# A two-layer diffusion block on one core: scan block copies in runs, the state decayed on GpSimd, adaLN vectors as products by rows

## The chip, the cores and the metric

The kernel runs on one core of one Trainium2 chip. Its engines are TensorE (PE, with its weight loads PEld), VectorE (DVE), ScalarE (ACT), GpSimd (POOL) and SyncE (SP), whose queue issues the DMAs. The metric is the device time of one execution in microseconds.

## The reference

The program computes two layers over 512 latent tokens and 256 context tokens of width 1024. Layer 0 mixes the tokens by a bidirectional RWKV-7 recurrence, layer 1 by a Hyena long convolution, and each layer has a SwiGLU feed-forward on either side. All of it is float32. Every sub-layer is steered by shift, scale and gate vectors (adaLN), nine per layer, which one linear map of SiLU(c) gives; in layer 0 the context has its own from SiLU(c_ctx).

```python
ml = [m[:, None, :] for m in jnp.split(jax.nn.silu(c) @ mod_w[i] + mod_b[i], 9, axis=-1)]
mc = jnp.split(jax.nn.silu(c_ctx) @ mod_w[i] + mod_b[i], 9) if ctx_live else None
xl = xl + 0.5 * ml[2] * _swiglu(_pre(xl, norm_g[i, 0], ml[0], ml[1]), ffn_w_gu[i, 0], ffn_w_down[i, 0])
...
def step(S, inp):
    w_t, k_t, v_t, kk_t, ka_t = inp[:5]
    sa = jnp.einsum('dbhvk,dbhk->dbhv', S, kk_t)
    S = S * w_t[..., None, :] - sa[..., None] * ka_t[..., None, :] + v_t[..., None] * k_t[..., None, :]
```

## The kernel before, in words

Activations lie transposed, features on the partitions. Each float32 product is made of three products of halves (`mm3`, lines 470 to 473): a weight block is loaded raw by SP (`wfetch`), split into `whi` on ACT and `wlo` on DVE (`split`, lines 476 and 477), and used by TensorE. The raw pool has two buffers, so SP issues a weight load when the block two before it has been split.

A feed-forward (`ffn`) goes through the hidden width in parts of 4 (first one) or 8 and 6 blocks. For each pair of hidden blocks TensorE makes gate and up products, ACT and DVE form `dh` and `dl`; then the part's down products are added into the residual `x` by DVE with the gate vector (line 594, and 647 in the page). PSUM has a pool of eight buffers. Between pairs and between down blocks `bg_step` advances the background work.

That work is the adaLN vectors but the first two: (layer, vector) (0,2) to (0,4) for both streams and (0,5) to (0,8) for latents in the first feed-forward, (1,0) to (1,4) in the second, (1,5) to (1,8) in the third. For one vector `mod_dve` loads eight blocks of 128 rows of the map into `mraw` (two buffers, `mod_raw`, line 373), and DVE adds each, scaled by the stream's SiLU(c), into an accumulator `macc` of 128x1024 (lines 406 and 408). Eight matmuls against a column of ones then sum the accumulator over the partitions (line 414; each is recorded twice) and `mod_place` adds the bias.

The recurrence runs in chunks of 64 tokens, 12 blocks of two chunks, both directions. In each block the triangular matrices `Bc` are copied block by block into `Dl` (`lanes`, ACT, line 1223), transposed in 32x32 squares on DVE into `L` (`lanes2`, 1227), inverted on DVE (1258, 1265), transposed back (`unlane`, 1277) and copied into `XT` (`unlane2`, ACT, 1288). The state `Sn` is carried by `carry`: DVE writes the decayed state into the operand `SV` of a later step (1337) and GpSimd then decays `Sn` itself (1338); `advance` adds the new part (1376). `scores` has its lower half masked by GpSimd (1175) after ACT copied it out (1174).

A scheduler that simulates the program orders most of it. In the first blocks of the scan PE, DVE and POOL keep the written order, later PE and DVE, and in the adaLN vectors of the start PE; each engine runs its instructions in the order so found, SP's DMA issues too.

## Time and profile before

| | us |
|---|---|
| three runs | 3077.65, 3083.25, 3086.89; median 3083.25 |
| profiled execution | 3075.51 |
| its span | 3073.7 |
| busy: PE, DVE, ACT, POOL | 2822.9, 1811.0, 1203.1, 434.7 |
| mean granted TensorE clock | 0.944 of 2.4 GHz |

The span counts from the first to the last instruction. A row of a view by line groups all instructions of one source line and shape; "idle before" is the time its engine sat still before them and what ended it. Waits are inferred, and an engine's idle time matters only where another waits for it.

### The profile page before, as it was taken

What the parts mean: (1) busy time and instruction counts of PE and PEld (TensorE: products, weight loads), DVE (VectorE), ACT (ScalarE), POOL (GpSimd) and SP (SyncE); (2) the same over time, 40 slices, a digit from 0 to 9 for tenths busy, and PEclk for the clock granted to TensorE, in tenths of its full rate; (3) what the DMA queues carried; (4) which work ended last, traced back from release to release, by engine and by line L of the source; (5) the groups of instructions that cost most, each with busy time, mean ns of one, the idle gap of its engine ahead of it and who ended that gap; (6) DMA issues with size and microseconds to landing.
All of it is one profiled execution on the core that took longest, in us unless ns stands there. A gap on an engine that the chain in (4) does not pass through costs nothing.

```text
span 3073.7 us, 46929 instructions
## 1 busy us (share of the span) xinstructions
PE 2822.9 (92%) x18698; PEld 2362.3 (77%) x18698; DVE 1811.0 (59%) x3253; ACT 1203.1 (39%) x2003; POOL 434.7 (14%) x515
## 2 busy tenths in 40 slices
PE   8999999968889577887899999999999989899998
PEld 4888888857666466766788889888887767888888
DVE  5744544373798678887745555454356578653334
ACT  3121121254667788884232223322234322242222
POOL 0000000032343445432100000000000044100000
PEclk9999999989999678889899999999999999999999
DMA  6533432312688734324535444354233444332231
GB/s 226 175 105 116 151 103 83 95 40 99 173 211 213 192 106 135 109 83 120 189 110 172 146 162 144 103 186 156 96 118 121 179 169 151 107 110 96 96 101 50
DMA packets 363394, 407.28 MB, mean 133 GB/s; under 512 B 77655, under 2 KB 303063, under 8 KB 361448
## 3 DMA queue, kind: packets, MB, share of 16 engines
q1 hardware_dynamic: 363176, 404.29, 42.0%
q8 instruction: 147, 2.41, 0.3%
q14 instruction: 71, 0.58, 0.1%
HBM read 338.10 MB, written 65.34 MB: 131 GB/s over the span
## 4 chain that ended last, share of the span: by engine, by line
PE 75%; DVE 11%; ACT 6%; DMA 4%; issue 3%; POOL 1%; SPq 0%; DVEq 0%; ACTq 0%; POOLq 0%
PE ps L471 21%; PE ps L473 21%; PE ps L472 21%; PE sc L1198 1%; PE ps L414 1%; ACT Dl L1223 1%; DVE wlo L477 1%; ACT XT L1288 1%; DVE Dl L1265 1%; ACT AG L1174 1%; DVE xm L743 1%; DVE Tm L1258 1%; PE pf L1747 1%; DVE SV L1337 1%; DVE zt L1934 1%
## 5 line engine op out<-in xcount | busy, mean ns | idle before, releaser
L472 PE MATMUL ps<-hl,whi 128*128 128x512 f32 (+1 forms) x2064 | 742.0, 362 | 3.8 <-DVE hl L265 3.7
L471 PE MATMUL ps<-hh,whi 128*128 128x512 f32 (+1 forms) x2064 | 733.0, 363 | 13.1 <-ACT hh L264 10.7
L473 PE MATMUL ps<-hh,wlo 128*128 128x512 f32 (+1 forms) x2064 | 735.9, 362 | 2.6 <-DVE wlo L477 2.6
L477 DVE TENSOR_TENSOR wlo<-raw,whi 128x1024 fp32r<-128x1024 f32 (+1 forms) x325 | 393.0, 1215 | 404.0 <-ACT whi L476 402.7
L476 ACT CAST whi<-raw 128x1024 fp32r<-128x1024 f32 (+1 forms) x338 | 344.7, 1028 | 719.4 <-PE ps L472 657.0
L471 PEld LDWEIGHTS ps<-hh,whi 128*128 128x128 f32 x2064 | 386.8, 191 | 76.9 <-ACT hh L264 13.3
L472 PEld LDWEIGHTS ps<-hl,whi 128*128 128x128 f32 x2064 | 392.6, 190 | 64.3 <-DVE hl L265 5.1
L473 PEld LDWEIGHTS ps<-hh,wlo 128*128 128x128 f32 x2064 | 391.6, 190 | 64.6 <-DVE wlo L477 3.7
L472 PE MATMUL ps<-dl,whi 128*128 128x512 f32 (+1 forms) x1072 | 357.6, 335 | 0.0
L473 PE MATMUL ps<-dh,wlo 128*128 128x512 f32 (+1 forms) x1072 | 356.9, 334 | 0.0
L471 PE MATMUL ps<-dh,whi 128*128 128x512 f32 (+1 forms) x1072 | 356.2, 336 | 0.0
L601 DVE TENSOR_TENSOR sg<-sg,ps 128x512 f32<-128x512 f32 (+1 forms) x110 | 69.2, 633 | 259.1 <-PE ps L473 249.8
L408 DVE SCALAR_TENSOR_TENSOR macc<-mraw,cs,macc 128x1024 f32<-128x1024 f32 x133 | 169.0, 1283 | 87.9 <-DMA mraw<-in_mod_w 87.2
L471 PEld LDWEIGHTS ps<-dh,whi 128*128 128x128 f32 x1072 | 203.3, 190 | 20.9
L473 PEld LDWEIGHTS ps<-dh,wlo 128*128 128x128 f32 x1072 | 203.7, 190 | 20.4
L472 PEld LDWEIGHTS ps<-dl,whi 128*128 128x128 f32 x1072 | 203.7, 190 | 20.0
L600 ACT ACTIVATE sg<-ps 128x512 f32<-128x512 f32 (+1 forms) x110 | 59.7, 553 | 228.9 <-PE ps L473 216.3
L476 ACT CAST dh<-sg 128x512 fp32r<-128x512 f32 (+1 forms) x110 | 62.4, 576 | 213.5 <-DVE sg L601 213.4
L1779 POOL TENSOR_SCALAR G<-G 128x512 f32<-128x512 f32 x8 | 11.9, 1492 | 938.2 <-ACT G L1770 920.5
L472 PE MATMUL ps<-xl,whi 128*128 128x512 f32 (+2 forms) x336 | 124.8, 373 | 11.5 <-DVE xl L798 6.7
L647 DVE SCALAR_TENSOR_TENSOR x<-ps,der,x 128x512 f32<-128x512 f32 (+1 forms) x128 | 82.4, 664 | 81.6 <-PE ps L473 81.5
L471 PE MATMUL ps<-xh,whi 128*128 128x512 f32 (+1 forms) x336 | 120.9, 372 | 9.8 <-ACT xh L805 6.5
(313 smaller groups left out, 4619.8 us busy)
## 6 DMA issues: line engine op xcount, KB each, us to landing
raw<-in_wgu SPq DMA_DIRECT2D x88, 1024.0 KB, 5.0
mraw<-in_mod_w SPq DMA_DIRECT2D x144, 512.0 KB, 4.3
raw<-in_wd SPq DMA_DIRECT2D x24, 1024.0 KB, 4.7
raw<-in_wrkv SPq DMA_DIRECT2D x12, 1024.0 KB, 5.7
S_A<-AR SPq DMA_DIRECT2D x32, 384.0 KB, 3.6
AG<-S_A SPq DMA_DIRECT2D x48, 256.0 KB, 4.4
KK<-S_K SPq DMA_DIRECT2D x24, 512.0 KB, 4.5
KL<-S_K SPq DMA_DIRECT2D x48, 256.0 KB, 2.9
```

Of the source, the lines that this page charges most:

```text
L408: nc.vector.scalar_tensor_tensor(acc, raw, sc, acc, ALU.mult, ALU.add)
L414: nc.tensor.matmul(pt[:, m : m + 1], acc[:, m * P : (m + 1) * P], self.ones, start=m == 0, stop=m == DT - 1)
L471: nc.tensor.matmul(out, wh, xh, start=start, stop=False)
L472: nc.tensor.matmul(out, wh, xl, start=False, stop=False)
L473: nc.tensor.matmul(out, wl, xh, start=False, stop=stop)
L476: self.nc.scalar.copy(hi, src)
L477: (self.nc.gpsimd if pool else self.nc.vector).tensor_tensor(lo, src, hi.bitcast(F32), ALU.subtract)
L600: nc.scalar.activation(sg, pg, AF.Silu)
L601: nc.vector.tensor_mul(sg, sg, pu)
L647: nc.vector.scalar_tensor_tensor(X[m][:, o : o + w], pt, gates[who][:, m : m + 1], X[m][:, o : o + w], ALU.mult, ALU.add)
L743: nc.vector.scalar_tensor_tensor(dst, src, self.pv(f"mix{j}")[:, mc], dst, ALU.mult, ALU.add)
L1174: nc.scalar.copy(dst, src)
```

## The change

The adaLN map's columns from the third vector on are handed over transposed (`mod_wt`), so that one row of 1024 inputs belongs to one output. `mod_rows` spreads SiLU(c) (and SiLU(c_ctx)) as a row over all partitions: a column copy on GpSimd, a DMA that repeats the row, and a Silu of 128x1024 on ACT, once per feed-forward with background work. `mod_dve` multiplies each block of 128 outputs by that row and sums along it in one DVE instruction, whose sums are a column of the vector; the matmuls against ones are gone. Each load waits for a one-column copy on GpSimd that reads `begun`, the last `dl` written. In the scan the copies to `Dl` and to `XT` run over 32 neighbours, and the two transposes take the permutation instead. GpSimd decays the state first, and DVE copies it to `SV`.

```diff
-        if (i, k) == (0, 2) and q < self.nmod:
-            self.nc.vector.tensor_copy(raw[:, :1], self.begun)
-        self.nc.sync.dma_start(raw, self.A["mod_w"][i, q * P : (q + 1) * P, k * D : (k + 1) * D])
+        if held is not None:
+            self.nc.gpsimd.tensor_copy(raw[:, :1], held)
+        self.nc.sync.dma_start(raw, src)
...
+    def mod_rows(self, whos):
+        nc = self.nc
+        self.rows = {}
+        for w in whos:
+            t = self.rows[w] = self.modp.tile([P, D], F32, tag=f"mc{w}", name=self.nm("mc"))
+            nc.gpsimd.tensor_copy(t[:, :1], self.begun)
+            nc.sync.dma_start(t, self.A["cv"][("l", "c").index(w) : ("l", "c").index(w) + 1].to_broadcast([P, D]))
+            nc.scalar.activation(t, t, AF.Silu)
...
-            raw = self.mod_raw(i, k, q)
-            for w, acc in zip(whos, accs):
-                sc = self.cs[:, q, (0 if w == "l" else 1)].unsqueeze(1)
-                if q == 0:
-                    nc.vector.tensor_scalar(acc, raw, sc, None, ALU.mult)
-                else:
-                    nc.vector.scalar_tensor_tensor(acc, raw, sc, acc, ALU.mult, ALU.add)
+            raw = self.mod_raw(self.A["mod_wt"][i, o : o + P], self.begun)
+            for j, w in enumerate(whos):
+                dst = raw
+                if j < len(whos) - 1:
+                    dst = self.modp.tile([P, D], F32, tag="mprod", name=self.nm("mprod"))
+                nc.vector.tensor_tensor_reduce(
+                    dst, raw, self.rows[w], 1.0, 0.0, ALU.mult, ALU.add, accum_out=cols[w][:, m : m + 1]
+                )
...
-        for w, acc in zip(whos, accs):
-            pt = self.ps(DT)
-            for m in range(DT):
-                nc.tensor.matmul(
-                    pt[:, m : m + 1], acc[:, m * P : (m + 1) * P], self.ones, start=m == 0, stop=m == DT - 1
-                )
-            self.mod_place(pt, w, i, k)
+        for w in whos:
+            self.mod_place(cols[w], w, i, k)
...
+                    self.begun = dl[-1][:, :1].bitcast(F32)
+                    if jp == 0 and self.bg:
+                        self.mod_rows(("l", "c") if first else ("l",))
                     self.bg_step(4 if first and j0 == 0 else 2)
...
-            BD = t["BD"] = Dl.rearrange("p a r -> p (a r)").rearrange("p (t c) -> p t c", c=16)
-                nc.scalar.copy(BD[r].rearrange("p t c -> p c t"), Bcc[r, :, b : b + 32])
+                nc.scalar.copy(Dl[r], Bcc[r, :, b : b + 32])
...
-                L.rearrange("p r (h c) -> p r h c", h=2), t["BD"].unsqueeze(2).to_broadcast([P, 32, 2, 16])
+                L.rearrange("p r (h c) -> p r h c", h=2),
+                Dl.rearrange("p c t -> p t c").unsqueeze(2).to_broadcast([P, 32, 2, 16]),
...
-            nc.vector.transpose(XD, Dl)
-            t["XD"] = XD.rearrange("p a (h c) -> p a h c", h=2)
+            nc.vector.transpose(XD.rearrange("p c (a h) -> p a h c", h=2), Dl.rearrange("p a (h c) -> p a h c", h=2))
...
-                nc.scalar.copy(XTc[r, :, b : b + 32], t["XD"][r].rearrange("p a h c -> p c (a h)"))
+                nc.scalar.copy(XTc[r, :, b : b + 32], t["XD"][r])
...
+            nc.gpsimd.tensor_tensor(Sn, Sn, pc.to_broadcast([P, NP, 64]), ALU.mult)
             for hh in range(2):
-                nc.vector.tensor_mul(SV[hr[hh], hh], Sn[hr[hh]], pc[hr[hh]].to_broadcast([64, NP, 64]))
-            nc.gpsimd.tensor_tensor(Sn, Sn, pc.to_broadcast([P, NP, 64]), ALU.mult)
+                nc.vector.tensor_copy(SV[hr[hh], hh], Sn[hr[hh]])
```

SP's queue at the first part of the first feed-forward, before: `raw` are weight blocks (`in_wd` the down projection's), `mraw` blocks of the adaLN map; 654 to 668 stand ahead of these rows, and the vector (0,2) ends with 928.

```order
L450 DMA raw_680<-in_wgu 128x8x256
L373 DMA mraw_916<-in_mod_w 128x1024
L450 DMA raw_690<-in_wd 128x4x256
L373 DMA mraw_920<-in_mod_w 128x1024
L373 DMA mraw_924<-in_mod_w 128x1024
L373 DMA mraw_928<-in_mod_w 128x1024
L373 DMA mraw_1018<-in_mod_w 128x1024
L373 DMA mraw_1022<-in_mod_w 128x1024
L450 DMA raw_958<-in_wd 128x4x256
L450 DMA raw_1030<-in_wd 128x4x256
L450 DMA raw_1100<-in_wd 128x4x256
L450 DMA raw_1170<-in_wgu 128x8x256
```

Now, with the vector (0,2) from 662 to 680 and from 930 to 948:

```order
L376 DMA mraw_668<-in_mod_wt 128x1024
L376 DMA mraw_674<-in_mod_wt 128x1024
L376 DMA mraw_680<-in_mod_wt 128x1024
L460 DMA raw_962<-in_wd 128x4x256
L460 DMA raw_1038<-in_wd 128x4x256
L460 DMA raw_1112<-in_wd 128x4x256
L460 DMA raw_1186<-in_wgu 128x8x256
L376 DMA mraw_930<-in_mod_wt 128x1024
L376 DMA mraw_936<-in_mod_wt 128x1024
L460 DMA raw_1266<-in_wgu 128x8x256
L376 DMA mraw_942<-in_mod_wt 128x1024
L376 DMA mraw_948<-in_mod_wt 128x1024
```

The second half of the vector's loads moved from in front of the second down block to behind the gate block of the next part, the last two behind one more weight block.

DVE's queue before, at the end of that part's last pair and the first down products (`mods` and `der` are the vector and the gate made of it, `ps_960` the first down product):

```order
L477 TENSOR_TENSOR dl_695<-sg_856,dh_694 128x512
L365 TENSOR_TENSOR mods<-ps_932,pv 128x8
L406 TENSOR_SCALAR macc_1016<-mraw_1018,cs 128x1024
L352 TENSOR_SCALAR der<-mods 128x8
L477 TENSOR_TENSOR wlo_1097<-raw_1030,whi_1096 128x1024
L477 TENSOR_TENSOR dl_695<-sg_911,dh_694 128x256
L408 SCALAR_TENSOR_TENSOR macc_1016<-mraw_1022,cs,macc_1016 128x1024
L365 TENSOR_TENSOR mods<-ps_943,pv 128x8
L406 TENSOR_SCALAR macc_1017<-mraw_1018,cs 128x1024
L352 TENSOR_SCALAR der<-mods 128x8
L408 SCALAR_TENSOR_TENSOR macc_1017<-mraw_1022,cs,macc_1017 128x1024
L647 SCALAR_TENSOR_TENSOR x_74<-ps_960,der,x_74 128x512
```

And now (the row `ISA mprod` or `ISA mraw` is the product with its sum, the row behind it writes the sum out):

```order
L487 TENSOR_TENSOR wlo_1259<-raw_1186,whi_1258 128x1024
L421 ISA mraw_942,mcol_661<-mraw_942,mc_656 128x1024
L421 ISA mcol_661 128x1
L421 ISA mprod_951,mcol_660<-mraw_948,mc_652 128x1024
L421 ISA mcol_660 128x1
L421 ISA mraw_948,mcol_661<-mraw_948,mc_656 128x1024
L421 ISA mcol_661 128x1
L368 TENSOR_TENSOR mods<-mcol_660,pv 128x8
L368 TENSOR_TENSOR mods<-mcol_661,pv 128x8
L355 TENSOR_SCALAR der<-mods 128x8 x2
L660 SCALAR_TENSOR_TENSOR x_74<-ps_964,der,x_74 128x512
```

The first addition into `x` was preceded by work on the next vector, and is now preceded by the last two blocks of its own.

DVE's queue in the scan before, from one sum into the state to the carry behind it, with what each waits for:

```order
L1376 TENSOR_TENSOR Sn_1413_8917<-pss_8323,Sn_1413_8917 128x256 [waits PE_49,Activation_49,Pool_49]
L1258 TENSOR_TENSOR Tm_1590_10557<-L_10456,Dl_10431 128x3x26 [waits DVE_49]
L1258 TENSOR_TENSOR Tm_1589_10556<-L_10456,Dl_10431 128x3x27
L1265 TENSOR_TENSOR Dl_10431<-Dl_10431,Tm_1590_10557 128x3x26 [waits DVE_49]
L1265 TENSOR_TENSOR Dl_10431<-Dl_10431,Tm_1589_10556 128x3x27 [waits DVE_49]
L1258 TENSOR_TENSOR Tm_1590_10557<-L_10456,Dl_10431 128x4x24 [waits DVE_49]
L1258 TENSOR_TENSOR Tm_1589_10556<-L_10456,Dl_10431 128x4x25
L1337 TENSOR_TENSOR SV_10633<-Sn_1413_8917,PC 64x256 [waits DMAHW2_49,DMAHW1_49]
L1337 TENSOR_TENSOR SV_10633<-Sn_1413_8917,PC 64x256
```

And now:

```order
L1388 TENSOR_TENSOR Sn_1429_8913<-pss_8319,Sn_1429_8913 128x256 [waits PE_49,Activation_49]
L1271 TENSOR_TENSOR Tm_1606_10553<-L_10452,Dl_10427 128x3x26 [waits DVE_49]
L1271 TENSOR_TENSOR Tm_1605_10552<-L_10452,Dl_10427 128x3x27
L1278 TENSOR_TENSOR Dl_10427<-Dl_10427,Tm_1606_10553 128x3x26 [waits DVE_49]
L1278 TENSOR_TENSOR Dl_10427<-Dl_10427,Tm_1605_10552 128x3x27 [waits DVE_49]
L1271 TENSOR_TENSOR Tm_1606_10553<-L_10452,Dl_10427 128x4x24 [waits DVE_49]
L1271 TENSOR_TENSOR Tm_1605_10552<-L_10452,Dl_10427 128x4x25
L1350 COPY SV_10629<-Sn_1429_8913 64x256 [waits DMAHW4_49,DMAHW3_49,Pool_49]
L1350 COPY SV_10629<-Sn_1429_8913 64x256
```

The order is the same; the write to `SV` is a copy that waits for GpSimd (`Pool_49`). GpSimd's queue around the same product before (`AG` and `Hu` are the score masks, four to a step):

```order
L1175 AFFINE_SELECT AG_9452<-AG_9452 64x512 [waits PE_49,Activation_49]
L1175 AFFINE_SELECT Hu_9687<-Hu_9687 64x256 [waits Activation_49]
L1175 AFFINE_SELECT AG_9452<-AG_9452 64x512 [waits Activation_49]
L1175 AFFINE_SELECT Hu_9687<-Hu_9687 64x256 [waits Activation_49]
L1129 MEMSET AG_10118 64x2x512 [waits DMAHW1_49,DMAHW0_49,PE_49]
L1129 MEMSET AG_10118 64x2x512
L1338 TENSOR_TENSOR Sn_1413_8917<-Sn_1413_8917,PC 128x256 [waits DVE_49,Pool_49]
```

And now:

```order
L1188 AFFINE_SELECT AG_9448<-AG_9448 64x512 [waits PE_49,Activation_49]
L1348 TENSOR_TENSOR Sn_1429_8913<-Sn_1429_8913,PC 128x256 [waits DVE_49,Pool_49]
L1188 AFFINE_SELECT Hu_9683<-Hu_9683 64x256 [waits Activation_49]
L1188 AFFINE_SELECT AG_9448<-AG_9448 64x512 [waits Activation_49]
L1188 AFFINE_SELECT Hu_9683<-Hu_9683 64x256 [waits Activation_49,Pool_49]
```

The product moved from behind the four masks and two zero fills of its step to behind the first mask.

## Rows read from the trace of the kernel before

**Rows 1.** Busy time by stretch: PE, PEld, DVE, ACT, POOL (instructions), TensorE clock, DMA share, GB/s.
```profile
50.00:700.00 650.00, 624.42 (x3581) 549.36 (x3580) 347.19 (x497) 169.67 (x259) 25.34 (x18) 0.97 0.34 106
1200.00:1260.00 60.00, 50.88 (x899) 42.29 (x897) 50.10 (x148) 53.28 (x107) 33.39 (x51) 0.91 0.43 131
```

**Rows 2.** Timeline of TensorE: start and length in us, instruction, idle before it.
```profile
367.04 1.84 PE L414 MATMUL ps<-ones,macc 128*128 128x1 f32 x16
368.75 0.47 PE L471 MATMUL ps<-hh,whi 128*128 128x512 f32 x1
```

**Rows 3.** Busy time by stretch around the column sums (columns as in rows 1).
```profile
152.70:157.20 4.50, 4.50 (x35) 4.50 (x34) 3.66 (x5) 1.05 (x1) 0.00 (x0) 0.80 0.60 205
157.20:162.20 5.00, 5.00 (x13) 3.94 (x14) 2.57 (x5) 0.00 (x0) 0.00 (x0) 0.50 0.58 163
246.80:252.00 5.20, 5.20 (x21) 4.27 (x21) 2.98 (x5) 0.00 (x0) 0.00 (x0) 0.67 0.69 202
368.90:374.00 5.10, 5.10 (x23) 4.20 (x24) 2.62 (x5) 0.00 (x0) 0.00 (x0) 1.00 0.47 132
```

**Rows 4.** Timeline of TensorE at 75 us (columns as in rows 2).
```profile
75.83 0.73 PE L473 MATMUL ps<-hh,wlo 128*128 128x512 f32 x2 [0.98 <-DVE wlo L477]
```

**Rows 5.** DVE by line: instruction and count | busy us, mean ns | idle before.
```profile
L408 DVE SCALAR_TENSOR_TENSOR macc<-mraw,cs,macc 128x1024 f32<-128x1024 f32 x133 | 169.0, 1283 | 87.9 <-DMA mraw<-in_mod_w 87.2
...
L1019 DVE TENSOR_TENSOR_SCAN q<-cst,q 128x390 f32<-128x390 f32 x32 | 35.2, 1100 | 1.3
...
L365 DVE TENSOR_TENSOR mods<-ps,pv 128x8 f32<-128x8 f32 x23 | 3.5, 160 | 0.3 <-PE ps L393 0.2
```

**Rows 6.** Timeline around the first down projection, all engines.
```profile
119.33 0.48 PE L471 MATMUL ps<-dh,whi 128*128 128x512 f32 x1
...
127.83 1.05 ACT L476 CAST whi<-raw 128x1024 fp32r<-128x1024 f32 x1 [9.21 <-PE ps L472]
```

**Rows 7.** DMA issues of the page: count, KB each, us from issue to landing.
```profile
mraw<-in_mod_w SPq DMA_DIRECT2D x144, 512.0 KB, 4.3
```

**Rows 8.** ACT by line (columns as in rows 5).
```profile
L1288 ACT COPY XT<-L 32x512 f32<-32x512 f32 x48 | 51.0, 1063 | 5.7 <-DVE L L1277 5.0
L1223 ACT COPY Dl<-Bc 32x512 f32<-32x512 f32 x48 | 50.7, 1056 | 0.7
...
L1231 ACT COPY Dl<-cst 128x512 f32<-128x512 f32 x12 | 7.4, 618 | 2.6 <-DVE L L1227 2.4
```

**Rows 9.** Chain of waits from 1075 to 1460 us, shares by line.
```profile
by line: PE sc L1198 10.2%; ACT Dl L1223 5.8%; issue 5.6%; ACT XT L1288 5.5%; DVE Dl L1265 5.1%; DVE Tm L1258 5.0%; DVE SV L1337 4.4%; PE pss L1345 3.9%; ACT AG L1174 3.8%; PE pss L1370 3.6%; PE pss L1360 3.3%; PE ps L1305 2.9%; DMA gr<-in_
```

**Rows 10.** Chain of waits from 1000 to 1075 us, shares by line.
```profile
by line: DMA AG<-S_A 17.3%; PE ps L1198 12.8%; ACT Dl L1223 11.1%; PE sc L1198 7.7%; issue 7.4%; ACT AG L1174 6.9%; ACT Bc L1206 5.2%; SPq L1130 2.6%; PE ps L1316 2.5%; POOL XT L1285 2.0%; ACT a L1017 1.9%; PE pss L1360 1.8%; DVE L L1227 1.
```

**Rows 11.** DVE by line in the scan and one copy (columns as in rows 5).
```profile
L1337 DVE TENSOR_TENSOR SV<-Sn,PC 64x256 f32<-64x256 f32 x88 | 43.3, 492 | 0.7
...
L1227 DVE STREAM_TRANSPOSE L<-Dl 128x1024 f32<-128x1024 f32 x12 | 14.9, 1243 | 14.0 <-ACT Dl L1223 14.0
...
L1277 DVE STREAM_TRANSPOSE L<-Dl 128x512 f32<-128x512 f32 x12 | 8.5, 710 | 0.3
...
L1780 DVE COPY G<-G 1x512 f32<-1x512 f32 x8 | 3.3, 411 | 5.6 <-POOL G L1779 5.6
```

**Rows 12.** Timeline of one carry in the scan, all engines.
```profile
1274.34 3.27 ACT L1288 COPY XT<-L 32x512 f32<-32x512 f32 x3
...
1275.91 0.42 DVE L1376 TENSOR_TENSOR Sn<-pss,Sn 128x256 f32<-128x256 f32 x1
...
1277.44 0.85 DVE L1337 TENSOR_TENSOR SV<-Sn,PC 64x256 f32<-64x256 f32 x2
...
1278.93 0.78 POOL L1175 TENSOR_SCALAR_AFFINE_SELECT AG<-AG 64x512 f32<-64x512 f32 x1 [3.67 <-ACT AG L1174]
...
1281.57 0.62 POOL L1338 TENSOR_TENSOR Sn<-Sn,PC 128x256 f32<-128x256 f32 x1
```

**Rows 13.** Timeline of DVE before the first down projection.
```profile
105.73 1.23 DVE L477 TENSOR_TENSOR wlo<-raw,whi 128x1024 fp32r<-128x1024 f32 x1 [7.96 <-ACT whi L476]
```

More of the change, by code (lines that the diff above doesn't have):

```diff
@@ L167, in host_arrays @@
     A["pv"] = np.concatenate([v[n].reshape(DT, P).T for n in _PV], axis=1)
-    A["mod_w"] = I["mod_w"]
+    A["mod_w"] = I["mod_w"][0, :, : 2 * D]
+    A["mod_wt"] = I["mod_w"].transpose(0, 2, 1)
+    A["cv"] = np.stack([I["c"][0], I["c_ctx"]])
     A["wgu"] = I["ffn_w_gu"].reshape(4, D, 2 * F)
@@ L366, in mod_place, with mod_raw @@
         self.mod_finish(who, i, k)
-    def mod_raw(self, i, k, q):
+    def mod_raw(self, src, held=None):
         raw = self.modp.tile([P, D], F32, tag="mraw", name=self.nm("mraw"), bufs=self.nmod)
-        if (i, k) == (0, 2) and q < self.nmod:
-            self.nc.vector.tensor_copy(raw[:, :1], self.begun)
-        self.nc.sync.dma_start(raw, self.A["mod_w"][i, q * P : (q + 1) * P, k * D : (k + 1) * D])
+        if held is not None:
+            self.nc.gpsimd.tensor_copy(raw[:, :1], held)
+        self.nc.sync.dma_start(raw, src)
         return raw
@@ L380, in mod_pe @@
         for q in range(DT):
-            raw = self.mod_raw(i, k, q)
+            raw = self.mod_raw(self.A["mod_w"][q * P : (q + 1) * P, k * D : (k + 1) * D])
             for n in range(2):
@@ L395, in mod_pe @@
             self.mod_place(pt[:, j::2], who, i, k)
+    def mod_rows(self, whos):
[6 more added lines that the diff above has]
+            nc.scalar.activation(t, t, AF.Silu)
     def mod_dve(self, i, k, whos):
         nc = self.nc
-        accs = [self.modp.tile([P, D], F32, tag=f"macc{w}", name=self.nm("macc")) for w in whos]
-        for q in range(DT):
-            raw = self.mod_raw(i, k, q)
-            for w, acc in zip(whos, accs):
-                sc = self.cs[:, q, (0 if w == "l" else 1)].unsqueeze(1)
-                if q == 0:
-                    nc.vector.tensor_scalar(acc, raw, sc, None, ALU.mult)
-                else:
-                    nc.vector.scalar_tensor_tensor(acc, raw, sc, acc, ALU.mult, ALU.add)
-            if q < DT - 1:
-                yield
-        for w, acc in zip(whos, accs):
-            pt = self.ps(DT)
-            for m in range(DT):
-                nc.tensor.matmul(
-                    pt[:, m : m + 1], acc[:, m * P : (m + 1) * P], self.ones, start=m == 0, stop=m == DT - 1
-                )
-            self.mod_place(pt, w, i, k)
+        cols = {w: self.modp.tile([P, DT], F32, tag=f"mcol{w}", name=self.nm("mcol")) for w in whos}
+        for m in range(DT):
+            o = k * D + m * P
+            raw = self.mod_raw(self.A["mod_wt"][i, o : o + P], self.begun)
[6 more added lines that the diff above has]
+                )
+            if m < DT - 1:
+                yield
+        for w in whos:
+            self.mod_place(cols[w], w, i, k)
         yield
@@ L1219, in lanes @@
             t["Dl"] = Dl = T([P, 16, 32], "Dl", 2)
-            BD = t["BD"] = Dl.rearrange("p a r -> p (a r)").rearrange("p (t c) -> p t c", c=16)
             for hb in range(4):
                 r, b = slice(hb * 32, hb * 32 + 32), (hb % 2) * 32
-                nc.scalar.copy(BD[r].rearrange("p t c -> p c t"), Bcc[r, :, b : b + 32])
+                nc.scalar.copy(Dl[r], Bcc[r, :, b : b + 32])
         def lanes2(t):
             L = T([P, 32, 32], "L", 2)
+            Dl = t["Dl"]
             nc.vector.transpose(
-                L.rearrange("p r (h c) -> p r h c", h=2), t["BD"].unsqueeze(2).to_broadcast([P, 32, 2, 16])
+                L.rearrange("p r (h c) -> p r h c", h=2),
+                Dl.rearrange("p c t -> p t c").unsqueeze(2).to_broadcast([P, 32, 2, 16]),
             )
-            Dl = t["Dl"]
             nc.scalar.copy(flat(Dl), self.c("id32"))
@@ L1275, in unlane @@
             L, Dl = t["L"]
-            XD = L[:, :16]
-            nc.vector.transpose(XD, Dl)
-            t["XD"] = XD.rearrange("p a (h c) -> p a h c", h=2)
+            t["XD"] = XD = L[:, :16]
+            nc.vector.transpose(XD.rearrange("p c (a h) -> p a h c", h=2), Dl.rearrange("p a (h c) -> p a h c", h=2))
         def unlane2(t):
```

## The prediction

> **What bounds the kernel now.** I read the busy time by stretches first, to see which engine each stage hangs on. In the first feed-forward and the token mixer's projections (50 to 700 us) TensorE is busy 624 of 650 us; in a piece of the scan (1200 to 1260) no engine is: ACT 53, PE 51 and DVE 50 of 60 us [rows 1]. So in the feed-forwards only TensorE's own work and what makes it wait counts, and in the scan three engines hand work round. The timeline of TensorE then shows what one adaLN vector costs it, the chain of waits which copies of the scan lie on the path, and the timeline of one carry how far GpSimd runs behind DVE (VectorE).
>
> **Column sums leave TensorE.** The old way ends each vector with eight f32 matmuls of accumulator columns against ones, recorded as 16. One such run starts at 367.04 and the next product at 368.75, on a TensorE that never idles there: 1.71 us [rows 2]. There are 19 vectors (three for both streams, four and nine for latents alone), so 19 x 1.7 = 32.3 us go. Runs of two vectors cost more: from 152.7 the granted clock is 0.80 for 4.5 us and then 0.50, that is 1.2 of 2.4 GHz, for 5.0 us; after the pair at 243 it is 0.67 for 5.2 us; after a single vector it stays 1.00 [rows 3]. Lost there: 0.9 + 2.5 + 1.7 = 5.1 us, and I count it as won. What is late next is the weight split on DVE, which costs TensorE nearly nothing now; one visible stall of 1.0 us at 75.8 [rows 4] lies behind accumulations that move away, and I count that too. Together -38 us.
>
> **Products by rows on DVE.** 152 multiply-and-reduce instructions of 128x1024 replace 133 accumulations of 1.28 us and 19 scalings. The trace of before has no such reduction. Bounds: 1.28 us (accumulation, same elements), and 2.9 us at the price of the scan instruction, 1100 ns for 390 elements [rows 5]. The program has a second small instruction behind each; a 128x8 addition takes 0.16 us [rows 5]. I take 1.28 + 0.16 = 1.44, since the nearest row has the same shape and as many operands. That is some 30 to 36 us more DVE time over stages where DVE has 300 us spare in the first 650 alone [rows 1]: hidden, save in one place.
>
> **The place: gate of the first feed-forward.** Its vector (0,2) is needed by the first down projection. Before, all its eight blocks were loaded ahead of the second weight block of that projection; now four stand behind three down blocks and a gate block in SP's queue, and the last two behind one more (the order rows). Call the first down product T (119.33 before). Two output blocks later ACT gets the next weight buffer, at 127.83 [rows 6], so one output block takes 4.25 us, and the PSUM pool's eight buffers hold four (two streams each): TensorE stops at T+17.0 unless DVE has begun to evacuate, which needs the gate. DVE's queue: split of the third down block ends at T+8.5+1.05+1.2 = T+10.8 (cast and split [rows 6, 13]); only then can SP issue the next weight block and, behind it, load 942, whose buffer the second product of 930 frees at T+12.2; 4.3 us to land [rows 7] and I add 0.5 for the 1 MB ahead of it: T+17. Then product 942a (18.4), a split of 1.24 that had to wait for TensorE's release at T+17 (to 20), 942b (21.4), 948a and b (24.3), four small ones (25), the first evacuation 0.75: T+25.7. A stall of about 9 us, plus 2 us for a clock at 0.50 after it (what the stretch at 0.50 lost [rows 3]). Lower end 0, if the loads land while the DVE is still at the splits; upper 16, if each wait repeats once. Taken: +11. Later vectors have no such deadline: they are wanted one sub-layer on. The held loads (one GpSimd column copy each) stand on GpSimd while it has nothing else in the feed-forwards, and the four ACT Silus of 128x1024 fall where ACT is under 30% busy (170 of 650 us [rows 1]).
>
> **Scan, block copies.** Eight ACT copies per block of 32x512 take 1.06 us each; a contiguous 128x512 copy on ACT takes 0.62 [rows 8]. Half of them lie on the path: 5.8% + 5.5% of the 385 us from 1075 to 1460, 43.5 us, and 11.1% of the 75 us before, 8.3 us [rows 9, 10]. A cut of 0.42 of 51.8 us is -21.6.
>
> In exchange the two DVE transposes of each block now walk in steps of 128 bytes: 1.24 and 0.71 us now [rows 11]. No row shows DVE at such a step. Bounds: nothing, and what ACT pays for its step of 64 bytes, 0.44 us per 512 elements, so 0.88 + 0.44 per block, 12 blocks, 16 us of DVE. I take the upper end, because ACT's row is the same data at a like step, and half of it on the path (DVE is busy 84% there): +8.
> The Trainium skill, page "Advanced Engine Details and Errata", section "Memory Cachelines", says that SBUF is read in lines of 16 bytes and that an access pattern which takes each element from another line pays for it. That speaks against moving the step to the DVE. ACT's rows agree (1.06 against 0.62 us); by the rule the term is the +8 above, without it the sum would be 8 us lower.
>
> **Scan, carry.** DVE multiplied the state by the decay twice (88 x 0.492 us); now it copies (88 instructions of the same shape), and waits for GpSimd's product, which used to follow. A DVE copy of 512 elements takes 0.41 [rows 11], so one of 256 lies between 0.21 and 0.41; at 0.30 DVE saves 17 us, of which 40% counts (line 1337 has 17 of its 43 us on the path, 4.4% of 385 [rows 9, 11]): -7. The wait: DVE's queue has a sum into the state, six small instructions, then the carry. GpSimd's product takes 0.62 and now stands behind the first score mask of the same step. One that comes late [rows 12]: sum ends 1276.3, carry 1277.4, the mask ends 1279.7, since ACT, held by the 4.3 us of block copies, fed it late; the copy would start at 1280.4, 3.0 us later. In this way seven of the 44 carries come 2.0 to 3.8 us late (20 us) and the rest together 11. The copies' cut makes ACT 1.8 us earlier in each of the seven: 31 - 13 = 18 us, 40% of it on the path: +7. Behind the waiting copy on DVE stand the inversion and the transposes for the next block, and TensorE waits for these. Scan: -21.6 + 8 - 7 + 7 = -14.
>
> **The sum.** -38 + 11 - 14 = -41 us. The profiled execution took 3075.5 us (span 3073.7), 7.7 below the median of 3083.25; so 3034 for one like it, and 3042 against the median.
>
> **Rivals.**
> (a) The hold costs nothing and the scan gains fully: the stall (11), the transposes (8) and the carry wait (7) fall away: 3042 - 26 = 3016. For it: DVE sits idle for 8.0 us before 105.7 [rows 13], so it has room for the first products; against: the order in SP's queue.
> (b) The scan gives nothing, since DVE, 84% busy, takes over what ACT loses: 3042 + 14 = 3056. For it: the three engines' shares are nearly equal [rows 1]. Against: half the copies are on the path.
> (c) The reduction is dear, 2.9 us: 80 of them in the first feed-forward add 128 us to DVE there, still under TensorE's time, but the chain to the first gate grows by 8 x 1.6 = 13 us, and I estimate 20 more from splits that come late: 3042 + 33 = 3075. For it: the trace lacks the instruction, and the scan is the only one in it that carries a sum along; against: the accumulation at one element per ns.
> (d) Slower: DVE becomes the bound of the scan. The carry waits of 31 us stay whole, the transposes cost 16 to 23 (the latter if both double [rows 11]) and the ACT copies turn out to be off the path: +54 there, -27 in the feed-forwards, 3110. It decides from 27 us of lengthening on. For it: a DVE that waits in order at 44 places; against: DVE waits for TensorE and ACT in that stretch already, and those waits absorb such lateness.
> That the column sums do not vanish can be left out: no instruction of that line is in the new program.
>
> **How the numbers follow.** Chances: forecast 0.48 (own range 3025 to 3058), (a) 0.17, (b) 0.19, (c) 0.09, (d) 0.07. A measurement of this kernel tells about 0.3%, 9 us, from no change. Faster by more than that means under 3074: forecast, (a), (b) and half of (c), less the forecast's and (b)'s tails of 0.03: 0.85; within it 0.08; slower 0.07. The range 3006 to 3074 leaves (d), half of (c) and the far end of (a) outside.
>
> **What would show it.** No matmul against ones and no clock of 0.50 after 157 us. A TensorE wait of some 9 us near 130 us, released by DVE's evacuation behind the gate: if absent, (a). The reduction at 1.2 to 1.5 us: if near 3, (c). Copies of line 1233 and 1300 at 0.6 us, transposes near 2.1 and 1.15, carry copies near 0.3. DVE's wait for GpSimd at the carry: about 18 us over the scan; above 40, with a longer scan, it is (d). The scan from first score to last state 14 us shorter; the forecast is wrong if it grows.

## The result and the profile after

| | before | after |
|---|---|---|
| median of four runs each, us | 3082.60 (3077.65 to 3086.89) | 3037.35 (3034.80 to 3039.90) |
| ratio | | 0.9854, 95% interval 0.9837 to 0.9871 |
| profiled execution, span | 3073.7 | 3035.0 |

The forecast was 3042, with a range of 3006 to 3074. A second set of runs on another chip gave 0.9841 (0.9826 to 0.9856), so the change saves 45 to 49 us, against 41 forecast.

Where the time went is read best at places that both programs pass. The table takes the start of one instruction at each from the two timelines.

| place | before | after | moved so far |
|---|---|---|---|
| first Silu of the first feed-forward | 64.2 | 66.7 | +2.6 |
| first DVE instruction of the projections | 590.2 | 580.2 | -10.0 |
| first score of the scan | 1004.6 | 1004.1 | -0.5 |
| last addition of the mixer's output | 1529.0 | 1504.4 | -24.6 |
| first matmul of the Hyena filters | 2288.5 | 2248.9 | -39.6 |
| end of the span | 3073.7 | 3035.0 | -38.7 |

The start is 2.6 us later: TensorE waits 10.4 us there for blocks of the map, 8.3 before. This place varies from 63.3 to 69.3 among the runs with the new start. The feed-forwards do what was forecast: -12.6 in the first one (forecast -17.1 - 5.1 - 1 + 11 = -12.2) and -15.1 in the second and third together (nine sums of 1.71, -15.4). Between them stand two surprises that cancel: the projections give back 9.5 us, and the scan with its output gains 24.1, not 14.

By stretch (columns as in [rows 1], of which these are the same two stretches), DVE is now the busiest engine in this piece of the scan, and ACT no longer is:

```profile
50.00:700.00 650.00, 617.72 (x3478) 540.79 (x3479) 351.14 (x578) 173.80 (x264) 51.29 (x77) 0.97 0.34 109
1200.00:1260.00 60.00, 51.51 (x930) 42.84 (x930) 53.81 (x157) 49.52 (x110) 31.42 (x49) 0.94 0.43 122
```

The first gate, in the timeline of DVE and TensorE. It answers to [rows 6, 13]:

```profile
126.06 1.23 DVE L421 CUSTOM_DVE_ANT_0 mprod<-mraw,mc 128x1024 f32<-128x1024 f32 x1 [5.60 <-DMA mraw<-in_mod_wt]
...
127.21 1.22 DVE L487 TENSOR_TENSOR wlo<-raw,whi 128x1024 fp32r<-128x1024 f32 x1
...
133.74 0.28 PE L483 MATMUL ps<-dh,wlo 128*128 128x256 f32 x1
...
134.77 1.23 DVE L421 CUSTOM_DVE_ANT_0 mprod<-mraw,mc 128x1024 f32<-128x1024 f32 x1 [2.79 <-DMA mraw<-in_mod_wt]
...
135.92 1.22 DVE L487 TENSOR_TENSOR wlo<-raw,whi 128x1024 fp32r<-128x1024 f32 x1
...
141.02 1.41 DVE L660 SCALAR_TENSOR_TENSOR x<-ps,der,x 128x512 f32<-128x512 f32 x2
...
141.82 0.79 PE L481 MATMUL ps<-dh,whi 128*128 128x512 f32 x1 [7.80 <-DVE x L660]
```

DVE stands idle 5.60 and 2.79 us for loads that were issued late, works through the products and one weight split between them, and evacuates the first block at 141.02. TensorE, whose next product needed the PSUM buffer that this evacuation frees, sat still for 7.80 us before 141.82. The last two numbers of the forecast's sum (9 and 2) are these 7.8 and the low clock behind it. In the next two rows, of the same kernel by stretch, the clock is 0.65 while TensorE is busy all 8 us, which is 2.8 us lost:

```profile
134.00:142.00 8.00, 0.20 (x2) 0.18 (x2) 7.19 (x15) 0.99 (x1) 1.25 (x2) 0.71 0.40 116
142.00:150.00 8.00, 8.00 (x30) 6.62 (x31) 7.27 (x14) 0.00 (x0) 1.05 (x1) 0.65 0.27 86
```

The new instructions by line (instruction and count | busy us, mean ns | idle before) answer to [rows 5]; the load's landing answers to [rows 7]:

```profile
L421 DVE CUSTOM_DVE_ANT_0 mraw<-mraw,mc 128x1024 f32<-128x1024 f32 x128 | 156.5, 1223 | 142.8 <-DMA mraw<-in_mod_wt 141.6
...
L375 POOL COPY mraw<-dl 128x1 f32<-128x1 f32 x128 | 44.8, 364 | 896.3 <-DVE dl L487 631.2 <-DVE mcol L421 260.5 <-DVE mods L368 4.5
...
L421 DVE DVE_READ_ACCUMULATOR2_ANT mcol<- 128x1 f32 x152 | 12.5, 82 | 0.0
```

```profile
mraw<-in_mod_wt SPq DMA_DIRECT2D x128, 512.0 KB, 5.3
```

One product costs 1.223 + 0.082 = 1.30 us (1.44 forecast). A load takes 5.3 us to land where it took 4.3.

The scan by line answers to [rows 8, 11]:

```profile
L1350 DVE COPY SV<-Sn 64x256 f32<-64x256 f32 x88 | 40.6, 462 | 11.2 <-POOL Sn L1348 9.8 <-DMA pv<-S_v 0.7
...
L1300 ACT COPY XT<-L 32x512 f32<-32x512 f32 x48 | 29.6, 616 | 14.0 <-DVE L L1290 13.3
L1235 ACT COPY Dl<-Bc 32x512 f32<-32x512 f32 x48 | 29.5, 615 | 0.7
...
L1240 DVE STREAM_TRANSPOSE L<-Dl 128x1024 f32<-128x1024 f32 x12 | 23.3, 1945 | 12.1 <-ACT Dl L1235 12.1
...
L1388 DVE TENSOR_TENSOR Sn<-pss,Sn 128x256 f32<-128x256 f32 x44 | 18.4, 419 | 12.7 <-PE pss L1382 7.8 <-ACT Bc L1219 4.1 <-ACT psq L1467 0.7
...
L1290 DVE STREAM_TRANSPOSE L<-Dl 128x512 f32<-128x512 f32 x12 | 12.9, 1072 | 0.3
```

The block copies went from 1.06 to 0.615 us as forecast, the transposes from 1.24 and 0.71 to 1.95 and 1.07 (2.12 and 1.15 forecast). The carry copies were forecast at 0.30 and take 0.46, and DVE waits 9.8 us for GpSimd there (18 forecast). The sum into the state (line 1388), which waits for TensorE's product, stands idle 12.7 us; before it was 36.5:

```profile
L1376 DVE TENSOR_TENSOR Sn<-pss,Sn 128x256 f32<-128x256 f32 x44 | 18.5, 421 | 36.5 <-PE pss L1370 33.6 <-ACT AG L1174 1.5 <-ACT psq L1455 0.8
```

The chain of waits in the scan, which answers to [rows 9], says the same: no block copy of ACT is left among its largest shares, and the carry copies, 4.4% as products, are at 7.3%.

```profile
by line: issue 10.4%; DVE Dl L1278 9.1%; DVE Tm L1271 8.0%; DVE SV L1350 7.3%; PE sc L1211 7.1%; DVE Dlo L1308 4.2%; PE ps L1317 3.8%; PE pss L1357 3.6%; PE pss L1382 3.4%; PE pss L1372 3.2%; PE ps L1174 3.2%; DVE L L1290 2.6%; DVE L L1240 
```

### The profile page after: what moved, and what is told of

Same layout as the page of the kernel before. It is cut to its first block, busy times and chain, and to the rows that moved or that the text cites. A ratio compares the mean times of both kernels' runs of the same rounds, so it can differ in the third digit from the quotient of the medians.

```text
span 3035.0 us, 46673 instructions
## 1 busy us (share of the span) xinstructions
PE 2782.4 (92%) x18394; PEld 2324.9 (77%) x18394; DVE 1818.3 (60%) x3403; ACT 1163.4 (38%) x2007; POOL 477.7 (16%) x647
## 4 chain that ended last, share of the span: by engine, by line
PE 74%; DVE 13%; DMA 4%; ACT 3%; issue 3%; POOL 2%; SPq 0%; DVEq 0%; POOLq 0%; ACTq 0%
PE ps L481 21%; PE ps L482 21%; PE ps L483 21%; DVE Dl L1278 1%; PE sc L1211 1%; DVE wlo L487 1%; DVE Tm L1271 1%; DMA mraw<-in_mod_wt 1%; DVE SV L1350 1%; DVE zt L1946 1%; POOL za L1947 1%; DVE zl L487 1%; PE pf L1759 1%; DMA AG<-S_A 1%; DMA x<-in_xT 1%
## 5 line engine op out<-in xcount | busy, mean ns | idle before, releaser
L421 DVE CUSTOM_DVE_ANT_0 mraw<-mraw,mc 128x1024 f32<-128x1024 f32 x128 | 156.5, 1223 | 142.8 <-DMA mraw<-in_mod_wt 141.6
L375 POOL COPY mraw<-dl 128x1 f32<-128x1 f32 x128 | 44.8, 364 | 896.3 <-DVE dl L487 631.2
L481 PE MATMUL ps<-xh,whi 128*128 128x512 f32 (+2 forms) x336 | 123.6, 380 | 9.5 <-issue 5.9
L483 PE MATMUL ps<-xh,wlo 128*128 128x512 f32 (+2 forms) x336 | 123.2, 372 | 0.0
```

What stands on the lines that cost most here:

```text
L375: self.nc.gpsimd.tensor_copy(raw[:, :1], held)
L421: nc.vector.tensor_tensor_reduce(dst, raw, self.rows[w], 1.0, 0.0, ALU.mult, ALU.add, accum_out=cols[w][:, m : m + 1])
L481: nc.tensor.matmul(out, wh, xh, start=start, stop=False)
L483: nc.tensor.matmul(out, wl, xh, start=False, stop=stop)
```

## The experiments

All ratios are to the kernel before, timed beside each run; 0.001 is 3 us, and an interval reaches 3 to 5 us to either side. The table gives, from each profile, the start of the projections and the length of three stretches: from there to the first score, from the first score to the last addition of the mixer's output, and from there to the first filter matmul. The start of the projections holds the variation of the start, so lengths say more than places.

| kernel | projections start | to first score | scan and output | feed-forwards 2, 3 | ratio |
|---|---|---|---|---|---|
| before | 590.2 | 414.4 | 524.4 | 759.6 | 1 |
| changed | 580.2 | 423.8 | 500.3 | 744.5 | 0.9854 |
| changed, again | 580.7 | 423.8 | 501.6 | 743.6 | 0.9841 |
| rows only | 581.2 | 421.4 | 515.8 | 743.4 | 0.9908 |
| scan only | 590.9 | 415.9 | 511.1 | 758.9 | 0.9972 |
| blocks only | 588.9 | 414.1 | 502.4 | 761.1 | 0.9920 |
| first pair | 573.1 | 421.1 | 512.4 | 743.5 | 0.9852 |
| old carry | 580.0 | 422.9 | 495.8 | 743.4 | 0.9842 |
| first pair, old carry | 577.0 | 422.2 | 506.4 | 743.5 | 0.9832 |
| carry on ACT | 576.9 | 422.3 | 506.6 | 743.6 | 0.9860 |
| sums back | 597.2 | 420.3 | 519.5 | 760.7 | 1.0008 |
| plain transposes | 580.5 | 426.0 | 491.0 | 743.1 | 0.9836 |
| hold first only | 594.0 | 420.0 | 507.1 | 753.8 | 0.9963 |

**The two halves.** Rows only: the changed kernel with `lanes`, `lanes2`, `unlane`, `unlane2` and `carry` of the kernel before. Scan only: the kernel before with these five of the changed one.

> The vectors by rows alone; block copies, transposes and carry of the scan as in the kernel before. Theory A (the parts add up, as the prediction has them): -38 + 11 = -27 us, about 3055. Theory B (the end of the mixer's projections is bound by its transfers, so what the first feed-forward wins is lost before the scan's first score, as the two traces show: -10 at the projections, -0.5 at the first score): only the 15 us of the second and third feed-forward remain, about 3067, and the first score stands within 2 us of 1004.6. Theory C (the 10 us are late at the first score but given back inside the scan, so the scan of the changed kernel gained 14 by itself and 10 from that): first score near 1004, end of the scan 10 us earlier than before, about 3056 in all.

> The scan's change alone (block copies, transposes, carry); vectors with column sums as before. The prediction's terms: -21.6 + 8 - 7 + 7 = -14, about 3069. Theory B: the scan itself gained the 24 us that lie between first score and scan end in the two traces: about 3059. Theory C: 14 us, about 3069.

Rows only came to 0.9908 (0.9895 to 0.9921), -28 us, where A said -27 and C nearly the same. B, at 3067, falls. What C said of the place holds too: the first score stands at 1002.7, so 7 of the 9 us won by the start of the projections are gone by then, and from there on the old scan code takes 515.8 us in place of 524.4. From the start of the projections to the mixer's end it is 937.2 against 938.8: no net change in code that was not touched. Scan only came to 0.9972 (0.9961 to 0.9983), -9 us: B's 24 fall, and the 14 of the parts lies just outside the interval (5 to 12 us). In its trace the same stretch takes 927.0, 11.8 less. So the 24 us of the changed kernel's scan are some 13 of its own (924.1 against 937.2) and a rest that pays back the projections. The loss before the first score is shared by all kernels with vectors by rows (420 to 426, against 414 to 416), and in all of them the scheduler put the projections' work in another order (by the traces some 210 of the 1640 TensorE products there stand at another place in the changed kernel than before, though no line of that stage was changed; scan only and blocks only keep the old order). That the order causes the loss is not shown.

**Block copies without the new carry.**

```diff
  # the kernel before, with lanes, lanes2, unlane, unlane2 of the changed one;
  # carry stays:
                 nc.vector.tensor_mul(SV[hr[hh], hh], Sn[hr[hh]], pc[hr[hh]].to_broadcast([64, NP, 64]))
             nc.gpsimd.tensor_tensor(Sn, Sn, pc.to_broadcast([P, NP, 64]), ALU.mult)
```

> The kernel before with the block copies and transposes of the changed one, and the carry as before. The prediction's terms: -21.6 + 8 = -13.6 us. With the whole scan change at -8.6 (ratio 0.9972) and the old carry 5 to 6 us better than the new one in the traces, this should come to -14, ratio 0.9954. Rival: block copies and carry are tied, the copies alone bring only the 8.6: ratio 0.9972.

The ratio is 0.9920 (0.9907 to 0.9933), -25 us: both answers were too small. The new carry, put on top of this (scan only), costs 16 us by the ratios and 10.5 by the traces (927.0 against 916.5). By line, first blocks only, then scan only:

```profile
L1336 DVE TENSOR_TENSOR SV<-Sn,PC 64x256 f32<-64x256 f32 x88 | 44.4, 504 | 0.7
...
L1375 DVE TENSOR_TENSOR Sn<-pss,Sn 128x256 f32<-128x256 f32 x44 | 18.4, 419 | 15.8 <-PE pss L1369 10.2 <-POOL AG L1175 3.5 <-ACT Bc L1206 1.0
```

```profile
L1337 DVE COPY SV<-Sn 64x256 f32<-64x256 f32 x88 | 40.9, 465 | 15.7 <-POOL Sn L1335 15.1
...
L1375 DVE TENSOR_TENSOR Sn<-pss,Sn 128x256 f32<-128x256 f32 x44 | 18.4, 419 | 11.2 <-PE pss L1369 7.4 <-ACT Bc L1206 2.3 <-ACT AG L1174 1.5
```

The sum into the state waits 10.2 us for TensorE where it waited 33.6 before. TensorE's own waits for ACT show why, in the two groups of products ahead of that sum; before, then blocks only:

```profile
L1360 PE MATMUL pss<-RHS,XT 64*64 64x64 f32 x768 | 39.6, 246 | 23.6 <-ACT XT L1318 15.4 <-ACT RHS L1347 8.0 <-POOL Sn L1338 0.2
...
L1370 PE MATMUL pss<-SV,KT 128*64 128x64 f32 x768 | 36.0, 242 | 18.0 <-ACT SV L1362 17.9
```

```profile
L1359 PE MATMUL pss<-RHS,XT 64*64 64x64 f32 x768 | 38.8, 244 | 13.0 <-ACT XT L1317 10.7 <-ACT RHS L1346 2.2
...
L1369 PE MATMUL pss<-SV,KT 128*64 128x64 f32 x768 | 35.4, 239 | 10.4 <-ACT SV L1361 10.4
```

ACT, freed of 42 us of copies, keeps TensorE waiting 18 us less at these two places, where TensorE waits for other instructions of ACT than the copies. The granted clock over scan and output rose too, from 0.82 to 0.86, and the same 6110 products kept TensorE busy for 394.7 us in place of 404.1; how much of the 25 us came by the clock, no run separates. The copies of the new carry save 3.5 us of DVE over the products (40.9 against 44.4), and the wait for GpSimd adds 15.1. But 5.0 of the 10.5 us come from an order of ACT at the end of the scan, shown below with the first gate.

**The old carry in the changed kernel, and the copies on ACT.**

```diff
-            nc.gpsimd.tensor_tensor(Sn, Sn, pc.to_broadcast([P, NP, 64]), ALU.mult)
             for hh in range(2):
-                nc.vector.tensor_copy(SV[hr[hh], hh], Sn[hr[hh]])
+                nc.vector.tensor_mul(SV[hr[hh], hh], Sn[hr[hh]], pc[hr[hh]].to_broadcast([64, NP, 64]))
+            nc.gpsimd.tensor_tensor(Sn, Sn, pc.to_broadcast([P, NP, 64]), ALU.mult)
```

> The changed kernel with the carry of the kernel before (DVE multiplies the state into SV, GpSimd decays it afterwards). The prediction priced the carry's change at -7 + 7 = 0: then 3037. Theory D (a DVE copy that runs beside GpSimd work takes 1.2 to 1.6 us a pair instead of 0.58, so the copies and their waits cost DVE 50 us against 44): 3 to 7 us faster than the changed kernel, 3030 to 3034. Rival: the decay on GpSimd, early as it is now, lets the sum into the state come early; without it the kernel is 5 us slower, 3042.

```diff
-                nc.vector.tensor_copy(SV[hr[hh], hh], Sn[hr[hh]])
+                nc.scalar.copy(SV[hr[hh], hh], Sn[hr[hh]])
```

> The changed kernel with the 88 carry copies on ACT instead of DVE. Theory D (a DVE copy slows down beside GpSimd work, and DVE is the busiest engine of the scan): DVE loses 40 us of copies and 10 of waits, ACT takes 88 x 0.37 = 33 us; 5 to 12 us faster than the changed kernel, about 3025 to 3030. Rival: ACT works through its queue in order, the copies wait there for GpSimd behind evacuations that TensorE waits for: same or up to 10 us slower.

With the old carry: 0.9842 (0.9828 to 0.9855), between the two values of the changed kernel, so the time alone can't tell 3 to 7 us from nothing; the trace has the stretch 6 us shorter (918.7 against 924.1 and 925.4 from projections to mixer's end), as D said. On ACT: 0.9860 (0.9846 to 0.9874), not faster, as its rival said. ACT's copies wait 14.1 us for GpSimd in ACT's queue, and the sum into the state is back at 34.0 us of waiting for TensorE:

```profile
L1350 ACT COPY SV<-Sn 64x256 f32<-64x256 f32 x88 | 35.5, 403 | 18.4 <-POOL Sn L1348 14.1 <-DMA KL<-S_K 3.2
...
L1388 DVE TENSOR_TENSOR Sn<-pss,Sn 128x256 f32<-128x256 f32 x44 | 18.6, 422 | 39.6 <-PE pss L1382 34.0 <-ACT XT L1300 2.9 <-ACT Bc L1219 1.0
```

**The first gate's wait.**

```diff
-                    self.begun = dl[-1][:, :1].bitcast(F32)
+                    if jp == 0 or not first or j0 > 0:
+                        self.begun = dl[-1][:, :1].bitcast(F32)
```

> The changed kernel, but all eight loads of the first vector wait for the first pair's dl instead of the second pair's, so that they stand ahead of the second down block in the DMA queue. Theory A: the 7.8 us of TensorE's wait before the first gate go, and up to 2 us of clock: 3028 to 3030. Theory B: the wait goes, and the projections' end gives it all back: 3037, no difference to the changed kernel. A rival: the loads push the down blocks back and TensorE waits for them instead, 3037 to 3040.

The wait is gone and the clock stays at 1.00 where it fell to 0.65:

```profile
134.00:142.00 8.00, 8.00 (x51) 7.21 (x50) 7.41 (x14) 2.10 (x2) 1.24 (x2) 1.00 0.41 147
142.00:150.00 8.00, 8.00 (x48) 7.07 (x47) 8.00 (x13) 1.05 (x1) 1.05 (x1) 1.00 0.78 263
```

The projections start 7 us earlier, the first score 10, and yet the ratio is 0.9852 (0.9837 to 0.9867): the scan gives it back (512.4 against 500.3). B named the wrong place, since the projections kept the gain. More than half of that loss stands at the end of the scan; first pair, then changed:

```profile
1428.73 1.99 ACT L486 CAST whi<-raw 128x1024 fp32r<-128x1024 f32 x2 [2.05 <-DMA raw<-in_wo]
1430.63 0.76 ACT L1375 ACTIVATE SV<-pss 64x256 f32<-64x256 f32 x2
...
1431.45 1.12 PE L1383 MATMUL pss<-SV,KT 128*64 128x64 f32 x16 [5.69 <-ACT SV L1375]
```

```profile
1432.20 0.77 ACT L1374 ACTIVATE SV<-pss 64x256 f32<-64x256 f32 x2
1434.23 1.04 ACT L486 CAST whi<-raw 128x1024 fp32r<-128x1024 f32 x1 [1.26 <-DMA raw<-in_wo]
...
1433.02 0.69 PE L1382 MATMUL pss<-SV,KT 128*64 128x64 f32 x16 [1.64 <-ACT SV L1374]
```

In first pair the scheduler put two weight casts of the output projection, with the wait for their load, ahead of the last evacuation `SV` in ACT's queue, and the last state products wait 5.69 us for it in place of 1.64. From that evacuation to the last addition of the output it then takes 76.0 us, against 72.2 in the changed kernel and 73.8 in its second run. Some 4 us more are lost between 1260 and 1400 us and stay open. The same two casts stand in front in scan only (6.6 us of waiting), sums back (6.3), carry on ACT (5.6) and first pair with the old carry (5.5); in all the other kernels `SV` comes first and the wait is 1.5 to 1.6. So 4 to 5 us of what these five lose in the scan are the price neither of the gate nor of the carry. This is read from the traces; no run changes that order alone.

> Both mends: the loads of the first vector wait for the first pair, and the carry is as in the kernel before. By the sum of parts 7.8 + 4 us faster than the changed kernel, about 3022 to 3026. Rival: the stall's 7 us are given back behind the projections, as the run with the first mend alone suggests: 3027 to 3030, like the old carry alone.

Both mends: 0.9832 (0.9819 to 0.9845), the fastest kernel of the study, but its interval overlaps the changed kernel's. Of the 12 us expected over the changed kernel, 3.7 came (3025.8 against 3029.5 for the changed kernel timed beside it), which is nearer to the rival. Here too the scan takes 10.6 us more than with the old carry alone (506.4 against 495.8).

**The holds.**

```diff
-            raw = self.mod_raw(self.A["mod_wt"][i, o : o + P], self.begun)
+            raw = self.mod_raw(self.A["mod_wt"][i, o : o + P], self.begun if (i, k) == (0, 2) else None)
```

> The changed kernel, with the hold on the loads of the first vector alone; the first gate's wait of 7.8 us stays. The scheduler then orders the projections as in the run that mended that wait (22 TensorE rows differ from the changed kernel). If that order is why the mended run lost 9 us between projections' start and the mixer's end (933.5 us against 924.1 and 925.4), this run loses them too: 933 there and 8 us slower than the changed kernel. If the loss came with the earlier start, 925 here and the same time as the changed kernel.

Neither: 0.9963 (0.9946 to 0.9980), 34 to 38 us slower than the changed kernel. The profiled execution is one of the two fastest of seven, so its trace holds only 20 to 25 of them: the first feed-forward takes 15 to 17 us more from its first Silu on (the projections start 13.3 later), and the other two take 10 more. The order of the projections is not what costs (420.0 + 507.1 = 927.1, against 933.5 for first pair), so what that run lost between 1260 and 1400 us stays open; at the end of the scan `SV` comes first here, which is 4.2 us of the difference. What the holds are worth shows in the timeline:

```profile
273.58 1.23 DVE L421 CUSTOM_DVE_ANT_0 mraw<-mraw,mc 128x1024 f32<-128x1024 f32 x1 [4.38 <-DMA mraw<-in_mod_wt]
...
275.13 1.22 DVE L487 TENSOR_TENSOR wlo<-raw,whi 128x1024 fp32r<-128x1024 f32 x1
...
276.40 0.50 PE L483 MATMUL ps<-hh,wlo 128*128 128x512 f32 x1 [3.83 <-DVE wlo L487]
```

DVE takes up a product whose load has not landed and stands 4.38 us; the weight split behind it ends late, and TensorE waits 3.83 us for it. It does so 6 times (us in total, times, longest), against 4 times and 2.4 us in the changed kernel:

```profile
PE ps L483 <- DVE wlo L487: 11.1, 6, 3.8
```

Two waits for `dh`, late in the same way behind products on DVE, take 7.7 us in the second and third feed-forward, and the first gate's wait is 10.5 us in place of 7.8.

**The column sums.**

```diff
         for w in whos:
+            pt = self.ps(DT)
+            for m in range(DT):
+                nc.tensor.matmul(
+                    pt[:, m : m + 1], self.rows[w][:, m * P : (m + 1) * P], self.ones, start=m == 0, stop=m == DT - 1
+                )
+            nc.vector.scalar_tensor_tensor(cols[w], pt, 0.0, cols[w], ALU.mult, ALU.add)
             self.mod_place(cols[w], w, i, k)
```

> The changed kernel itself once more, beside the others of this call. If its projections' end and scan are a property of the program, the value projection takes 99 to 102 us again (94.9 before) and the scan from first score to last sum 430 +- 2; if the 430 was a chance of one execution, the scan takes 436 to 440, as in the two runs with the same scan code (438.5 and 439.5).

> The changed kernel with the matmuls against ones put back behind each vector, on the row tile, their result times zero added to the sums. The prediction's price for them is 32.3 us + 5.1 of clock: 33 to 38 us slower than the changed kernel, about 3070. Rival: TensorE has idle gaps where they fit, or they cost only their 0.9 us of instruction time: 10 to 17 us slower, about 3050. Second rival, for the 7 us that the projections' end lost: if these come from the order in which the scheduler puts the projections' work, this program, which has a third order there, shows another length from projections' start to the first score (before 414.4, rows 421 to 424); if they come from the row products themselves, 421 to 424 again.

The changed kernel, run again, repeats itself within 1.4 us in every stretch of the table, so the lengths belong to the programs. With the sums back the ratio is 1.0008 (0.9998 to 1.0019), 51 us slower than the changed kernel beside it. Of these, 16.5 lie in the first feed-forward (597.2 against 580.7, ten sums; 18.5 from the first Silu on) and 17.1 in the other two (760.7 against 743.6, nine): 33.6 to 35.6 us, 1.77 to 1.88 for each, where the forecast had 1.70 without its clock and 1.97 with it. Another 14.4 lie in the mixer (939.8 against 925.4), which holds no sums; 4.6 of them are the wait at the end of the scan. The projections stand in a third order here and take 420.3 us to the first score, which decides nothing on the order.

```profile
L429 PE MATMUL ps<-ones,mc 128*128 128x1 f32 x304 | 35.9, 246 | 0.0
```

**The transposes' step.**

```diff
-                nc.scalar.copy(Dl[r], Bcc[r, :, b : b + 32])
+                nc.scalar.activation(Dl[r], Bcc[r, :, b : b + 32], AF.Copy, scale=1e-6)
...
-                Dl.rearrange("p c t -> p t c").unsqueeze(2).to_broadcast([P, 32, 2, 16]),
+                flat(Dl).rearrange("p (t c) -> p t c", c=16).unsqueeze(2).to_broadcast([P, 32, 2, 16]),
...
-            nc.vector.transpose(XD.rearrange("p c (a h) -> p a h c", h=2), Dl.rearrange("p a (h c) -> p a h c", h=2))
+            nc.vector.transpose(XD, Dl)
```

> The changed kernel with the scan's two transposes per block walking over neighbours, as before the change, and the Dl copies scaled by 1e-6; the permutation of the block's lanes is left out, so the scan computes something else with the same instructions. The prediction priced the longer step at 16 us of DVE and +8 us of time; the trace of the changed kernel shows 12 x (0.70 + 0.36) = 12.8 us of DVE. Expected by the prediction's share of one half: 6 to 8 us faster than the changed kernel, about 3025. Rival: all of the 12.8 us lie on the path, since DVE is the busiest engine of the scan: 12 to 14 us faster. Second rival: TensorE's and ACT's waits absorb them: within 3 us.

```profile
L1240 DVE STREAM_TRANSPOSE L<-Dl 128x1024 f32<-128x1024 f32 x12 | 14.9, 1240 | 12.5 <-ACT Dl L1235 12.5
...
L1290 DVE STREAM_TRANSPOSE L<-Dl 128x512 f32<-128x512 f32 x12 | 8.5, 710 | 0.3
...
L1388 DVE TENSOR_TENSOR Sn<-pss,Sn 128x256 f32<-128x256 f32 x44 | 18.5, 420 | 15.5 <-PE pss L1382 11.8 <-ACT Bc L1219 3.6
```

This kernel leaves the permutation out, so only its time counts. The transposes are back at 1.24 and 0.71 us. Scan and output take 491.0 us, 9 to 11 less, of which 2.2 are lost before the first score: 7 to 8 us, half to two thirds of the 12.8. The ratio, 0.9836 (0.9819 to 0.9852), is lower by 2 to 5 us, too little to separate the answers. The run also settles a doubt on the state sum: with the longer transposes gone, DVE is busy for 387.0 us of scan and output (398 with its waits for GpSimd at the carry), less than the 404.8 of before, and yet the sum waits only 11.8 us for TensorE. So that wait did not fall because DVE had more work ahead of the sum.

## Why the prediction held, point by point

- *Column sums, -32.3 and -5.1 of clock.* Held: 33.6 to 35.6 us when put back by themselves, and the first feed-forward gained 12.6 us where the sum with clock and gate gives 12.2.
- *The reduction at 1.44 us.* Held, 1.30. Rival (c) is out.
- *First gate, +11.* Held at its place: 7.8 + 2.8 = 10.6. As a term of the total it fell: without the wait the kernel is not measurably faster, because the scan then takes 11 to 12 us longer. Of these, 4 us are the wait behind two weight casts at the end of the scan and 2 to 4 come behind it; the rest is open. Rival (a), a hold that costs nothing, is out at this place.
- *Products hidden in DVE's spare time.* True only because the loads are held. The prediction saw the holds as a cost; without the later ones the kernel is 34 to 38 us slower.
- *Block copies, -21.6, and transposes, +8.* The first was mis-sized. Together they were forecast at -13.6 and measure -25 (22 by the trace); with the transposes at 7 to 8 us the copies are worth some 30 of the 42 us that ACT lost, about three quarters and not one half. The chain's share counted only copies that stood on it. TensorE waits 18 us less for other instructions of ACT, and its clock is higher; both are in the measured sum and in no term of the forecast.
- *Carry, -7 + 7 = 0.* This step failed. A copy by itself takes 0.29 us, as forecast, but the sum had no term for copies beside GpSimd's work: the mean is 0.46, DVE saves 2.7 us [rows 11], not 17, and it waits 10 to 15 where 18 were forecast. In the changed kernel the new carry costs 6 us by the traces, too little for the times to show; put on top of the block copies alone it costs 10 to 16, of which 5 are the order at the end of the scan.
- *Scan, -14.* Held by compensation: -25 and +10 to +16 make -9 alone, and -13 in the changed kernel against rows only. Rivals (b) and (d), a scan that gains nothing or grows, are out.
- *The sum.* The parts give -28 - 9 = -37 and the whole 45 to 49. The 8 to 12 us between lie in the mixer, where untouched code differs by as much from one program to the next. Some 5 of them are the order at the end of the scan, which scan only has and the changed kernel has not; what sets the rest is open. That 41 stands so near to 45 to 49 is in part luck: the gain by the block copies was taken some 11 us too small, and the cost of the carry 6 to 16 us too small.

## What to carry to other kernels

A chain of waits prices an instruction only where it stands on the chain itself; on an engine that works in order, what it holds up behind it counts too, and here the cut on ACT was worth more than its share said. When work moves to an engine with spare time, ask what stands behind it in that engine's queue when its data is late: holding such loads back until their consumer's turn was worth 34 to 38 us here, more than the 28 that the vectors by rows won as a whole. And with a scheduler in between, code that nobody touched moved by 10 us either way: a gain seen at its own place can be gone at the end of the program, and a loss need not be the edit's own. Compare the queues first; two casts ahead of one evacuation were 4 to 5 us here.
